# RWKV-7 chain beside attention: the triangular solves of a head pair as one block-diagonal product, and the PSUM bank it leaves given to attention scores

## The chip, the cores and the metric

The kernel runs on one core of a Trainium2 chip. The metric is the device time of one execution in microseconds (us); the median of three executions of the kernel before is 2586.62 us. The engines of a core are called here as the profile calls them: PE (matmuls) with PEld (loads of the stationary operand), DVE, ACT, POOL, and SP, which in this kernel only starts DMA transfers.

## The reference, cut

One layer over 512 latent tokens with 256 context tokens ahead of them: a differential attention of 8 heads and a bidirectional RWKV-7 of 16 heads read the same projected input, are merged, and a PEER layer (retrieval of single-neuron experts) follows. The change concerns the recurrence of RWKV-7 and, by the order of the program, the attention that runs beside it.

```python
def wkv_scan(s0, scan_in):                      # per direction d and head h, 64 x 64 state s
    def step(s, inp):
        w, kk, a, k, v, r = inp
        sa = jnp.einsum('dbhij,dbhj->dbhi', s, kk)
        s = s * w[..., None, :] - sa[..., :, None] * (kk * a)[..., None, :] + v[..., :, None] * k[..., None, :]
        return s, jnp.einsum('dbhij,dbhj->dbhi', s, r)
    return lax.scan(step, s0, scan_in)
...
def one_block(q_blk):                           # attention, 128 queries, all 768 keys
    s = jnp.einsum('bmhqd,bmhkd->bmhqk', q_blk, k).astype(jnp.float32) * scale
    p = jax.nn.softmax(s, axis=-1)
    pd = (p[:, 0] - lam * p[:, 1]).astype(v.dtype)
    return jnp.einsum('bhqk,bhkd->bhqd', pd, v)
...
s_ctx, y_c = wkv_scan(s0, scan_c)               # 256 context tokens, then 512 latent ones
_, y_x = wkv_scan(s_ctx, scan_x)
```

## The kernel before

The program runs in stages: RWKV projections and the operands of the recurrence, pair of heads by pair (to about 715 us), then the recurrence and the attention together (about 743 to 1092 us), the merge of the branches, and PEER to the end.

**The chain.** `rwkv_chain` works through the recurrence in 24 steps of 32 tokens (8 of context, 16 of latent tokens), both directions at once. The 16 heads are 8 pairs; j is the head of a pair, d the direction, and the pairs form two groups g of four. One step has two half-steps, one for each group. A half-step consists of

- `reads` (matmuls L653): 16 products of 128x32 (stationary, from `cb`) with 128x64 (moving, from `sv`) into the bank `ps_r`; ACT copies it to `rhs` (L656);
- `solve` (L663): 16 products of 128x32 (from `XTz`) with 128x64 (`rhs`) into two banks, `ps_u0` and `ps_u1`, one for each j; ACT copies the first to the rows of `sv` that belong to it (L666), DVE the second (L667);
- `state` (L675): 16 products of 128x64 (from `KBt`) with 128x64 (`sv`) into `ps_s`; DVE multiplies it into the `sv` of the next step in two pieces (L681);
- from step 8 on `outputs` (L694, 16 products like those of `reads`, copied by ACT at L697) and `collect` (L705, two transposes, added into `y`).

`XTz` holds the inverse of the triangular system of each pair, head and direction, 32x32, written in stage 1 by `rw_inverse` to `xD`. For each of the four (j, d) there is a tile of 128 rows by 32 columns that is zero outside of its 32 rows, so that a product with all 128 rows of `rhs` gives one solve. `cb` and `KBt` have two buffers, `XTz` two, `sv` three. `load(c + 1)` stands behind the solve of group 0 and `outputs(1, c - 1)`: `cb` and `KBt` are loaded from the SP queue (L637), `sv` (L642) and `XTz` (L644, four loads of 32 rows by 1 KB) from the POOL queue.

**The attention.** A unit is one head and one block of 128 queries: 32 units. `probs` computes four score tiles of 128x384, each from two matmuls (L785, L786) into a bank of the pool `atp` (two banks); DVE scales each into `p` (L788), ACT takes the exponentials (L790). `combine` scales and subtracts (L798 ACT, L800 DVE), transposes six blocks (L804) which ACT copies to `pdT` (L805), and multiplies them with the values (L808, six matmuls). The heads' q and k come through `kr`, `qr`, `va` (`att_load`, POOL queue). Of the 32 units the first 25 take the output bank of the pool `atq`, the last 7 that of `atr`, which opens when the pool of the chain's banks, `psc`, is closed.

**The order.** The two are written one after the other; a scheduler merges them into one fixed order for each engine, by its own model of times. Each engine then runs its row of instructions in that order. A matmul that stands early in PE's row holds up all behind it if its operands are late.

## Time and profile before

| what | value |
|---|---|
| median of 3 executions | 2586.62 us (2585.44 to 2592.0) |
| the profiled execution, its own time | 2591.84 us |
| its span in the trace | 2590.1 us |
| mean granted clock of PE | 0.976 |
| PE busy over the span | 2411.5 us, 93% |
| DVE, ACT, POOL busy | 2025.8 us (78%), 1184.6 us (46%), 482.8 us (19%) |

The profiled execution is 5.2 us above the median. Times of instructions below count from the start of the span. A busy share is an average over stages with different limits, so the stretch of the chain is read by itself: in the rows below it is cut into five pieces at beginnings of steps of the chain. A line of a timeline gives start, duration, engine, line of the program, operation, output and inputs, size, and, where there was any, the idle time before and what ended it. The matmuls of PE overlap, so the time that one takes of PE is read from its start to the start of the next. For the float32 operands here PE runs each matmul as two passes; "x32" in a row are the passes of 16 matmuls, while the transposes are one pass each.

### The profile page before, as it was taken

To read this page: it belongs to the slowest core of one execution; us is meant where nothing else is said; L and a number is where in the kernel's file an instruction comes from. 1 tells how busy PE (TensorE), PEld (TensorE's weight loads), DVE (VectorE), ACT (ScalarE), POOL (GpSimd) and SP (SyncE) were. 2 spreads that over 40 slices of the span, in tenths; PEclk is the share of its full clock that TensorE was granted. 3 is DMA by queue.
4 is the path that set the end of the run, shared out by engine and by line. 5 is a ranking of instruction groups with operands and counts; after the bars stand their busy time and mean duration, and the time that the engine had idled before them with its cause. 6 is when DMAs were issued, how large, how long until landed. Compare 5 with 4: busy or idle time off the path is not lost.

```text
span 2590.1 us, 46535 instructions
## 1 busy us (share of the span) xinstructions
PE 2411.5 (93%) x18109; PEld 2078.5 (80%) x18109; DVE 2025.8 (78%) x3919; ACT 1184.6 (46%) x2171; POOL 482.8 (19%) x518
## 2 busy tenths in 40 slices
PE   6999999899979999899899989998999999988898
PEld 3778778798967878668688979997888998866777
DVE  5779998977748767774499998775778888788894
ACT  4666666633336666652344444552333333323332
POOL 0000000000043333000000000013444444444430
PEclk8999999999989999999899999999999999999999
DMA  5367756787487766235432536779899999899983
GB/s 226 95 164 197 185 149 167 185 264 246 136 210 209 186 175 180 81 102 166 131 109 85 176 130 232 268 284 366 313 336 336 340 339 339 324 363 372 358 327 101
DMA packets 310349, 579.75 MB, mean 224 GB/s; under 512 B 83761, under 2 KB 197041, under 8 KB 303345
## 3 DMA queue, kind: packets, MB, share of 16 engines
q1 hardware_dynamic: 253040, 387.09, 46.6%
q0 software_dynamic: 45808, 155.61, 17.5%
q10 hardware_dynamic: 11280, 34.08, 4.1%
q8 instruction: 142, 2.33, 0.4%
q14 instruction: 79, 0.64, 0.1%
HBM read 470.93 MB, written 105.38 MB: 223 GB/s over the span
## 4 chain that ended last, share of the span: by engine, by line
PE 62%; DVE 20%; DMA 9%; ACT 4%; issue 4%; SPq 0%; POOL 0%; ACTq 0%; DVEq 0%; POOLq 0%
PE ps_v L1143 6%; PE ps_v L1145 6%; PE ps_v L1142 6%; PE ps_a L80 5%; PE ps_a L78 5%; PE ps_a L79 5%; PE pp L79 3%; PE pp L80 3%; PE pp L78 3%; PE ps_s L675 2%; PE ps_br L79 2%; PE ps_br L80 2%; PE ps_br L78 2%; DMA cb<-cbD 2%; PE ps_o L808 2%
## 5 line engine op out<-in xcount | busy, mean ns | idle before, releaser
L78 PE MATMUL ps_a<-h,u_hi 128*128 128x384 f32 x1024 | 346.2, 338 | 10.0 <-ACT u_hi L69 10.0
L80 PE MATMUL ps_a<-h,u_lo 128*128 128x384 f32 x1024 | 347.2, 339 | 7.0 <-DVE u_lo L72 6.7
L79 PE MATMUL ps_a<-h,u_hi 128*128 128x384 f32 x1024 | 344.2, 336 | 0.0
L1080 POOL DMA_INDIRECT gr<-in_peer_u,ei x128 | 165.4, 1292 | 693.1 <-PE ps_a L79 472.5
L69 ACT CAST u_hi<-u_raw 128x1024 fp32r<-128x1024 f32 x128 | 134.3, 1051 | 289.8 <-PE ps_a L79 274.1
L72 DVE TENSOR_TENSOR u_lo<-u_raw,u_hi 128x1024 fp32r<-128x1024 f32 x128 | 156.3, 1221 | 102.4 <-ACT u_hi L69 101.1
L1080 POOL DMA_INDIRECT gr<-in_peer_v,ei x128 | 179.8, 1405 | 203.7 <-DVE ra L1098 182.6
L78 PEld LDWEIGHTS ps_a<-h,u_hi 128*128 128x128 f32 x1024 | 192.8, 188 | 16.1 <-ACT u_hi L69 13.7
L80 PEld LDWEIGHTS ps_a<-h,u_lo 128*128 128x128 f32 x1024 | 192.7, 188 | 12.7 <-DVE u_lo L72 11.6
L79 PEld LDWEIGHTS ps_a<-h,u_hi 128*128 128x128 f32 x1024 | 192.7, 188 | 2.4
L1098 DVE SCALAR_TENSOR_TENSOR ra<-gr,wk,ra 128x1024 f32<-128x1024 f32 x127 | 162.7, 1281 | 2.6 <-DMA gr<-in_peer_v,ei 1.5
L95 ACT CAST w_hi<-w_raw 128x1024 fp32r<-128x1024 f32 (+1 forms) x93 | 106.9, 1149 | 125.1 <-PE ps_br L79 59.3
L96 DVE TENSOR_TENSOR w_lo<-w_raw,w_hi 128x1024 fp32r<-128x1024 f32 (+1 forms) x93 | 125.0, 1344 | 49.5 <-ACT w_hi L95 43.8
L1087 DVE CUSTOM_DVE_ANT_0 gr<-gr,ht 128x1024 f32<-128x1024 f32 x128 | 153.8, 1219 | 11.2 <-DMA gr<-in_peer_u,ei 11.2
L1143 PE MATMUL ps_v<-v_lo,pw_hi 128*128 128x512 f32 x420 | 145.0, 403 | 12.0 <-DVE v_lo L1133 12.0
L1142 PE MATMUL ps_v<-v_hi,pw_hi 128*128 128x512 f32 x420 | 128.5, 400 | 16.0 <-ACT v_hi L1132 16.0
L546 PE MATMUL pp<-At,kz 128*128 128x128 f32 x768 | 106.2, 295 | 35.7 <-DVE kz L539 15.4
L78 PE MATMUL pp<-hx,w_hi 128*128 128x512 f32 x336 | 134.9, 402 | 3.4 <-ACT sgw L433 2.4
L80 PE MATMUL pp<-hx,w_lo 128*128 128x512 f32 x336 | 134.1, 399 | 2.0 <-DVE w_lo L96 2.0
L79 PE MATMUL pp<-hx,w_hi 128*128 128x512 f32 x336 | 133.0, 396 | 1.8 <-DVE hx L231 1.8
L1145 PE MATMUL ps_v<-v_hi,pw_lo 128*128 128x512 f32 x420 | 134.1, 401 | 0.0
L546 PEld LDWEIGHTS pp<-At,kz 128*128 128x128 f32 x768 | 98.4, 207 | 42.9 <-ACT kt L550 18.5
(374 smaller groups left out, 6390.7 us busy)
## 6 DMA issues: line engine op xcount, KB each, us to landing
u_raw<-in_uT SPq DMA_DIRECT2D x128, 512.0 KB, 4.6
v_raw<-in_peer_v SPq DMA_DIRECT2D x70, 512.0 KB, 8.3
w_raw<-in_peer_v SPq DMA_DIRECT2D x58, 512.0 KB, 6.5
wm<-in_w_mod SPq DMA_DIRECT2D x24, 1024.0 KB, 8.8
cb<-cbD SPq DMA_DIRECT2D x48, 512.0 KB, 6.5
gD<-gstage SPq DMA_DIRECT2D x12, 2048.0 KB, 8.3
gg<-gD SPq DMA_DIRECT2D x16, 1536.0 KB, 13.4
actD<-act SPq DMA_DIRECT2D x18, 768.0 KB, 3.6
```

The costliest lines, as they stand in the source:

```text
L69: nc.scalar.copy(hi, raw)
L72: (lo_eng or nc.vector).tensor_tensor(lo, raw, hi.bitcast(F32), op=OP.subtract)
L78: mm(ps, lh[0], rh[0], start=first, stop=False)
L79: mm(ps, lh[0], rh[1], start=False, stop=False)
L80: mm(ps, lh[1], rh[0], start=False, stop=last)
L546: nc.tensor.matmul(ps[:, c, :], kz[:, c, :], at, start=True, stop=True)
L1080: nc.gpsimd.indirect_dma_start(out=r, out_offset=None, in_=self.A[name], in_offset=bass.IndirectOffsetOnAxis(ap=self.ei[:, k:k + 1], axis=0))
L1087: nc.vector.tensor_tensor_reduce(out=r, in0=r, in1=self.ht, scale=1.0, scalar=0.0, op0=OP.mult, op1=OP.add, accum_out=w[:, k:k + 1])
L1098: nc.vector.scalar_tensor_tensor(self.ra, r, w[:, k:k + 1], self.ra, op0=OP.mult, op1=OP.add)
L1142: mm(pc[t][d], w[0][:, ts], v[0][:, c[d]], start=first, stop=False)
L1143: mm(pc[t][d], w[0][:, ts], v[1][:, c[d]], start=False, stop=False)
L1145: mm(pc[t][d], w[1][:, ts], v[0][:, c[d]], start=False, stop=last)
```

## The change

The four solves of a pair, (j, d) in all four combinations, become one product: `XTz` is now a tile in which the four 32x32 inverses of a pair stand on a block diagonal, 128x128, and `solve` has four matmuls of 128x128 with 128x64 instead of 16 of 128x32 with 128x64. The result goes to one PSUM bank, `ps_u`, in which each (j, d) has 32 rows of its own. [...] All that writes or reads operands in that order follows: the order of the halves in `kz`, the rows of `tt`, the mask (built on the host), the loads of `sv`. The two copies of 32x512 out of the solve's banks become four of 32x256, two on ACT (d = 0) and two on DVE (d = 1).

The loads of `XTz` go from 32 rows of 1 KB in one piece to 32 rows of 8 pieces of 128 bytes. The stores of `tt` to `tD` in stage 1 double in number (96 instead of 48, half the size each).

The bank that becomes free goes to the scores: `atp` has three instead of two. `atr`, which opens with the merge, has two instead of three.

```diff
@@ rw_scores
-                            eng.tensor_tensor(zo[:, :, 0, ::-1], zi[:, :, 0], w[1][h, g4], op=OP.mult)
-                            eng.tensor_tensor(zo[:, :, 1], zi[:, :, 1], w[1][h, g4], op=OP.mult)
+                            eng.tensor_tensor(zo[:, :, 1, ::-1], zi[:, :, 0], w[1][h, g4], op=OP.mult)
+                            eng.tensor_tensor(zo[:, :, 0], zi[:, :, 1], w[1][h, g4], op=OP.mult)
...
-                q2 = slice(64 * j + 32, 64 * j + 64)
-                nc.sync.dma_start(tD[j, cc].rearrange("c a d s t -> s (c a d) t"),
-                                  tt[q2].rearrange("p c d t -> p (c d) t"))
+                for dr in range(2):
+                    q = slice(64 * j + 32 - 32 * dr, 64 * j + 64 - 32 * dr)
+                    nc.sync.dma_start(tD[j, cc, :, dr].rearrange("c a s t -> s (c a) t"), tt[q, :, dr])
@@ rwkv_chain
-        clear = lambda j, i: nc.gpsimd.memset(sv[j][i][96 - 64 * j:128 - 64 * j], 0.0)
+        vrow = lambda j, d: slice(64 - 64 * j + 32 * d, 96 - 64 * j + 32 * d)
+        urow = lambda j, d: slice(96 - 64 * j - 32 * d, 128 - 64 * j - 32 * d)
+        clear = lambda j, i: [nc.gpsimd.memset(sv[j][i][urow(j, d), d], 0.0) for d in range(2)]
-        XTz = [mk(f"XTz{i}", [128, 4, 8, 32]) for i in range(NL)]
+        XTz = [mk(f"XTz{i}", [128, 8, 4, 32]) for i in range(NL)]
...
-                    nc.gpsimd.dma_start(sv[j][i][64 - 64 * j:96 - 64 * j, d], self.vTD[t:t + 32, j])
+                    nc.gpsimd.dma_start(sv[j][i][vrow(j, d), d], self.vTD[t:t + 32, j])
-                nc.gpsimd.dma_start(XTz[c % NL][32 * q:32 * q + 32, q], self.xD[q // 2, c, q % 2])
+                nc.gpsimd.dma_start(XTz[c % NL][32 * q:32 * q + 32, :, 3 - q], self.xD[q // 2, c, q % 2])
...
         def solve(g, c):
-            pu = [self.psc.tile([128, 2, 4, 64], F32, name=f"ps_u{j}") for j in range(2)]
-            for dp in range(8):
-                for j in range(2):
-                    q, ur = 2 * j + dp % 2, 96 - 64 * j
-                    nc.tensor.matmul(pu[j][ur:ur + 32, dp % 2, dp // 2, :], XTz[c % NL][:, q, 4 * g + dp // 2, :],
-                                     rhs[g][:, dp // 2, :], start=True, stop=True)
+            pu = self.psc.tile([128, 4, 64], F32, name="ps_u")
+            for a in range(4):
+                nc.tensor.matmul(pu[:, a, :], XTz[c % NL][:, 4 * g + a].rearrange("p u t -> p (u t)"), rhs[g][:, a, :],
+                                 start=True, stop=True)
             G = slice(4 * g, 4 * g + 4)
-            nc.scalar.copy(sv[0][c % NS][96:128, :, G], pu[0][96:128])
-            nc.vector.tensor_copy(sv[1][c % NS][32:64, :, G], pu[1][32:64])
+            for j in range(2):
+                nc.scalar.copy(sv[j][c % NS][urow(j, 0), 0, G], pu[urow(j, 0)])
+                nc.vector.tensor_copy(sv[j][c % NS][urow(j, 1), 1, G], pu[urow(j, 1)])
@@ mixers
-        with self.pool("atp", 2, space=PSUM) as psS, self.pool("atq", 1, space=PSUM) as psO:
+        with self.pool("atp", 3, space=PSUM) as psS, self.pool("atq", 1, space=PSUM) as psO:
...
-                    self.pool("atr", 3, space=PSUM) as psR:
+                    self.pool("atr", 2, space=PSUM) as psR:
```

With these, the scheduler merges chain and attention in another order. The rows below are from the engines' orders; a name's number only tells buffers apart. Lines of the changed program stand three to four higher than before: the score matmuls are L789 and L790, transposes L808, value matmuls L812, reads L657, solve L666, state L679, outputs L698, collect L709.

PE, the second half of step 6 (a context step) before, from the end of the solve of group 1 to the first read of step 7:

```order
L663 MATMUL ps_u_8201<-rhs,XTz_6681 32x64
L663 MATMUL ps_u_8202<-rhs,XTz_6681 32x64
L808 MATMUL ps_o<-va,pdT 128x128 x6
L785 MATMUL ps_s<-kh,q_11246 128x384
L786 MATMUL ps_s<-kl_7297,q_11246 128x384
L785 MATMUL ps_s<-kh,q_11246 128x384
L786 MATMUL ps_s<-kl_7297,q_11246 128x384
L653 MATMUL ps_r<-sv_6688,cb_8149 32x64
```

PE, the second half of a dense context step of the changed program, from its last read to the middle of its `state` pieces:

```order
L657 MATMUL ps_r<-sv_6737,cb_7953 32x64
L679 MATMUL ps_s<-sv_7378,KBt_6732 64x64
L808 MATMUL ps_o<-c_ident,p_11084 128x128 x3
L679 MATMUL ps_s<-sv_7381,KBt_6734 64x64
L679 MATMUL ps_s<-sv_7378,KBt_6732 64x64
L789 MATMUL ps_s<-kh,q_10978 128x384
L790 MATMUL ps_s<-kl_7348,q_10978 128x384
L812 MATMUL ps_o<-va,pdT 128x128 x6
L789 MATMUL ps_s<-kh,q_10978 128x384
L790 MATMUL ps_s<-kl_7348,q_10978 128x384
L679 MATMUL ps_s<-sv_7381,KBt_6734 64x64
```

Before, a context step from 4 to 8 holds five score pairs, two to three groups of three transposes and one group of six value matmuls; now eight, four and two, and `state` is cut into pieces of 1, 2 and 13 by them.

PE, the end of a late step before, outputs of one group to the first read of the next step:

```order
L694 MATMUL ps_r<-sv_6689,cb_10007 32x64
L785 MATMUL ps_s<-kh,q_12070 128x384
L786 MATMUL ps_s<-kl_7297,q_12070 128x384
L804 MATMUL ps_o<-c_ident,p_12176 128x128 x3
L675 MATMUL ps_s<-sv_6688,KBt_6684 64x64
L785 MATMUL ps_s<-kh,q_12070 128x384
L786 MATMUL ps_s<-kl_7297,q_12070 128x384
L705 MATMUL ps_r<-c_ident,yt 128x128 x2
L653 MATMUL ps_r<-sv_6688,cb_10184 32x64
```

The same place of a late step now:

```order
L698 MATMUL ps_r<-sv_6737,cb_9676 32x64
L698 MATMUL ps_r<-sv_6735,cb_9675 32x64
L698 MATMUL ps_r<-sv_6737,cb_9676 32x64
L679 MATMUL ps_s<-sv_6736,KBt_6732 64x64
L709 MATMUL ps_r<-c_ident,yt 128x128 x2
L657 MATMUL ps_r<-sv_6736,cb_9831 32x64
```

From step 18 on the chain runs without attention between its products (one score pair in steps 18 to 22, where there were about six units). Up to the end of step 3 there are 18 value matmuls instead of 12, up to the end of step 9 there are 90 instead of 48, up to the end of step 17 150 instead of 102; when the chain ends 150 stand behind it in both, and 117 score pairs instead of 112.

ACT, in a dense context step now: the second copy of a solve, `sv_6738`, stands behind a copy of transposed probabilities that itself stands behind the first.

```order
L670 COPY sv_6736<-ps_u 32x256
L809 COPY pdT<-ps_o 128x384
L660 COPY rhs<-ps_r 128x256
L809 COPY pdT<-ps_o 128x384
L670 COPY sv_6738<-ps_u 32x256
L761 CAST kh<-kr 128x1536
```

Before, one copy took both directions, and nothing stood between.

## Rows read from the trace of the kernel before

**Rows 1.** The page's part 4: shares of the span on the chain of waits.

```profile
PE 62%; DVE 20%; DMA 9%; ACT 4%; issue 4%; SPq 0%; POOL 0%; ACTq 0%; DVEq 0%; POOLq 0%
```

**Rows 2.** Windows: length, busy PE, PEld, DVE, ACT, POOL; PEclk, DMA share, GB/s.

```profile
743.00:804.35 61.35, 44.80 (x862) 37.36 (x852) 34.61 (x68) 27.20 (x50) 23.40 (x44) 0.89 0.88 226
804.35:858.80 54.45, 53.85 (x1109) 44.91 (x1107) 47.51 (x103) 38.37 (x86) 24.16 (x49) 1.00 0.85 218
858.80:982.26 123.46, 112.46 (x2602) 95.00 (x2601) 82.97 (x180) 76.50 (x190) 44.77 (x88) 0.99 0.68 185
982.26:1056.00 73.74, 72.39 (x1711) 62.57 (x1710) 54.92 (x134) 47.36 (x108) 16.85 (x34) 0.98 0.51 149
1056.00:1092.00 36.00, 31.26 (x192) 24.41 (x192) 25.39 (x68) 26.87 (x67) 0.00 (x0) 1.00 0.23 74
```

**Rows 3.** Timeline of ACT: the `rhs` copy that opens steps 4, 18 and 23.

```profile
804.35 0.37 ACT L656 COPY rhs<-ps_r 128x256 f32<-128x256 f32 x1
...
982.26 0.37 ACT L656 COPY rhs<-ps_r 128x256 f32<-128x256 f32 x1 [2.08 <-PE ps_r L653]
...
1046.55 0.38 ACT L656 COPY rhs<-ps_r 128x256 f32<-128x256 f32 x1
```

**Rows 4.** Timeline of PE: context step 5, and step 19 from reads to outputs.

```profile
815.81 1.09 PE L663 MATMUL ps_u<-rhs,XTz 128*32 128x64 f32 x32
816.82 0.45 PE L785 MATMUL ps_s<-kh,q 128*128 128x384 f32 x1
...
817.28 0.49 PE L804 MATMUL ps_o<-c_ident,p 128*128 128x128 f32 x3
...
823.39 1.60 PE L808 MATMUL ps_o<-va,pdT 128*128 128x128 f32 x12
...
995.88 0.65 PE L653 MATMUL ps_r<-sv,cb 128*32 128x64 f32 x32
996.46 1.15 PE L675 MATMUL ps_s<-sv,KBt 128*64 128x64 f32 x32
997.54 0.55 PE L804 MATMUL ps_o<-c_ident,p 128*128 128x128 f32 x3
...
999.27 0.63 PE L694 MATMUL ps_r<-sv,cb 128*32 128x64 f32 x26
```

**Rows 5.** Timeline of PEld: one load of 128 columns, and two in a row.

```profile
816.82 0.19 PEld L785 LDWEIGHTS ps_s<-kh,q 128*128 128x128 f32 x1
...
823.39 0.30 PEld L808 LDWEIGHTS ps_o<-va,pdT 128*128 128x128 f32 x2
```

**Rows 6.** Timeline of SP's queue: the `cb` loads of steps 19 and 23.

```profile
988.02 0.80 SPq L637 DMA_DIRECT2D cb<-cbD  x2
...
1037.12 1.19 SPq L637 DMA_DIRECT2D cb<-cbD  x2
```

**Rows 7.** DMA issues from 804.35 to 1056: count, KB each, median us to landing.

```profile
cb<-cbD SPq DMA_DIRECT2D x36, 512.0 KB, 6.5
```

**Rows 8.** DMA issues from 1036 to 1044, the last step's loads.

```profile
cb<-cbD SPq DMA_DIRECT2D x2, 512.0 KB, 4.8
```

**Rows 9.** Lines by form, 743 to 1092, DVE, ACT, POOL: busy us, mean ns | idle before.

```profile
L681 DVE TENSOR_TENSOR sv<-ps_s,pcall 64x512 f32<-64x512 f32 x92 | 63.2, 687 | 24.5 <-PE ps_s L675 23.1
L667 DVE COPY sv<-ps_u 32x512 f32<-32x512 f32 x48 | 32.8, 684 | 23.9 <-PE ps_u L663 22.5
L666 ACT COPY sv<-ps_u 32x512 f32<-32x512 f32 x48 | 27.8, 579 | 37.5 <-PE ps_u L663 37.2
L656 ACT COPY rhs<-ps_r 128x256 f32<-128x256 f32 x48 | 17.6, 369 | 21.9 <-PE ps_r L653 17.0 <-DMA qTD<-zt 4.6
L644 POOL DMA_DIRECT2D XTz<-xD x88 | 43.4, 500 | 69.0 <-PE ps_u L663 67.8 <-DMA sv<-vTD 0.9 <-issue 0.2
L751 POOL DMA_DIRECT2D kr<-kTD x14 | 8.3, 598 | 15.2 <-DVE kl L758 15.0 <-issue 0.2
```

**Rows 10.** The page's part 5: gathers issued by POOL in PEER, 128 rows each.

```profile
L1080 POOL DMA_INDIRECT gr<-in_peer_u,ei x128 | 165.4, 1292 | 693.1 <-PE ps_a L79 472.5
```

More of the change, by code (lines that the diff above doesn't have):

```diff
@@ L547, in rw_scores @@
                     for j in range(2):
-                        q = slice(64 * j + 32, 64 * j + 64)
+                        q = slice(64 * j + 32 - 32 * dr, 64 * j + 64 - 32 * dr)
                         nc.scalar.copy(tt[q, c4, dr], ps[q, :, 0:32])
@@ L554, in rw_scores @@
             for j in range(2):
-                q2 = slice(64 * j + 32, 64 * j + 64)
-                nc.sync.dma_start(tD[j, cc].rearrange("c a d s t -> s (c a d) t"),
-                                  tt[q2].rearrange("p c d t -> p (c d) t"))
+                for dr in range(2):
+                    q = slice(64 * j + 32 - 32 * dr, 64 * j + 64 - 32 * dr)
+                    nc.sync.dma_start(tD[j, cc, :, dr].rearrange("c a s t -> s (c a) t"), tt[q, :, dr])
             for dst, src in ((self.cbD[:, 64:192], bt), (self.KBD, kt)):
@@ L1419, in layout @@
     lt, le = (i[:, None] < i[None]).astype(np.float32), (i[:, None] <= i[None]).astype(np.float32)
-    A["mask"] = c(np.stack([np.tile(np.block([[a, b], [0 * lt, le]]), (2, 1))
-                            for a, b in ((lt, le), (lt[::-1], le[::-1]))], axis=1))
+    A["mask"] = c(np.stack([np.tile(np.block(m), (2, 1))
+                            for m in ([[lt, le], [0 * lt, le]], [[0 * lt, le], [lt[::-1], le[::-1]]])], axis=1))
     A["smask"] = c(np.broadcast_to((np.arange(T) % 32 != 0).astype(np.float32), (128, T)))
```

## The prediction, on record before the changed kernel ran

> **What bounds the kernel now.** I read the chain of waits first: 62% of the span is PE, 20% DVE, 9% DMA [rows 1], so that work taken off PE or put on it counts where PE is full. The chain's 349 us I then read in five windows [rows 2]. From 743 to 804 PE is busy 44.8 of 61.4 us while DMA runs at a share of 0.88 and 226 GB/s: loads set the end, and PE has room. In steps 4 to 8 PE is busy 53.85 of 54.45 us, in steps 9 to 17 112.5 of 123.5, from step 18 to the end of the chain 72.4 of 73.7. In the tail it has 4.7 us of room again. A step takes 54.45 / 5 = 10.9 us from 4 to 8, 123.46 / 9 = 13.7 from 9 to 17, and (1046.55 - 982.26) / 5 = 12.9 from 18 to 22 [rows 2, 3]. So the question is not how much faster a solve is, but from where to where the attention moves: out of a stretch where PE is full into others.
>
> **A solve on PE.** Now 16 matmuls take 1.01 us (815.81 to 816.82 [rows 4]), the same number of the same shape in `reads` 0.58 (995.88 to 996.46). Reads go in turn to four bands of 32 output rows, solves to two. By that, a matmul of 64 moving columns costs its own band 0.126 (1.01 / 8) to 0.145 us (0.58 / 4), and four that fill all bands 0.50 to 0.58. Against this stands the load of the stationary operand. Two loads of 128 columns with nothing between them span 0.30 us, a single one 0.19, so one follows another by 0.11 [rows 5]. Four float32 matmuls are eight passes: 8 x 0.11 = 0.88 us. Six matmuls with 128 moving columns take at most 1.60 us [rows 4], 0.267 each, so four with 64 cost no more than 1.07. Bounds 0.50 and 1.07; I take 0.88, since a pass on 64 columns (about half of 0.126) is too short to hide a load of 0.11. Saving 0.13 for a half-step, bounds +0.51 and -0.06.
>
> [...]
>
> **The copies.** One of 32x512 costs 579 ns on ACT and 684 on DVE; one of 256 elements a row 369 on ACT [rows 9]. Two of 256 on ACT are then 0.74, on DVE, taken at 0.40 to 0.42 each by ACT's ratio of the two sizes, 0.82. That adds 0.16 us on ACT and 0.14 on DVE per half-step, 7.5 us in 48 half-steps. It also puts the second copy of ACT behind whatever stands between, in dense steps a `pdT` copy. `state` waits for it, which is why its pieces come as 1, 2 and 13: each cut costs PE about 0.2 us, as pieces overlap less (a passage of 1 or 2 matmuls keeps its own fill and drain). In stretches full of attention these waits are covered by score and value matmuls; in steps 18 to 22 only by outputs and collect.
>
> **The attention that moves.** A pair of score matmuls costs PE 0.46 us (816.82 to 817.28), three transposes 0.3 to 0.5, six value matmuls 1.54 (at most 1.60), reads 0.58, state 1.08, outputs about 0.59 [rows 4]. I sum five stretches.
>
> - A, 743 to step 4: one more unit's values and twelve more score pairs, 12 x 0.46 + 1.54 + 0.3 = 7.4 us of PE work, in a stretch with 16.5 us of room [rows 2] that loads leave. But one more head must be loaded by then, and scores of head 1 wait for it. +4, between -2 and +8.
> - B, steps 4 to 8: per step three more score pairs (1.4), one or two more groups of transposes (0.5), six more value matmuls (1.54), two cuts more (0.4 to 0.5), two cheaper solves (-0.26): 3.7 us, and at the present 1.04 to 1.07 of time over priced work 3.9. PE has no room there, so 5 x 4.0 = +20. DVE's bound is a little lower: its busy time in the five windows adds up to 245.4, less the chain's 63.2 + 32.8 that is 149 for 32 units, 4.7 each [rows 2, 9]; two units 9.3, state 4 x 0.687, copies 4 x 0.41 make 13.7. So a step goes from 10.9 to between 13.7 (+14 in all) and 16.5 (+28), where neither engine hides the other's waits.
> - C, steps 9 to 17: step 9 holds twelve value matmuls instead of six, steps 10 to 17 hold 60 instead of 54, with eight more score pairs and four more groups of transposes: 12/6 x 1.54 + 8 x 0.46 + 4 x 0.35 = 8.2, less 18 cheaper solves (2.3), is 5.9 us, with 11 us of room [rows 2] of which some is waits that stay. Half of it on the path: +3, between -6 and +8.
> - D, step 18 to the end of the chain: some 33 us of attention are gone, and 72.4 us of PE work become about 40. The step does not fall with it, for the loads of `cb` then set it. They have two buffers: a load starts when `outputs` of step c - 1 is done and must land before `reads` of c + 1. From first issue to last landing it takes 0.8 to 1.2 (the two issues) plus 4.8 (last step, nothing else under way) to 6.5 us (the median) [rows 6 to 8], so 5.6 to 7.5; I take 6.5. Then reads, state, solve, outputs in a row: 0.58 + 1.08 + 0.88 + 0.59 and cuts and starts, 3.5 us (4.05 now, 995.88 to the end of outputs [rows 4]). 10.0 a step instead of 12.9, so 5 x -2.9 = -14.5; the last step, 9.45 now, falls by 0.5. -15, between -7 and -23 (8.4 a step, PE's own work and the copies' waits).
> - E, the tail: five score pairs fewer, 5 x 0.46; two output banks instead of three in `atr` take some back. -2, between -3 and +3.
>
> Sum: 4 + 20 + 3 - 15 - 2 = **+10 us**. The profiled execution, 2591.84, would become 2601.8; the median 2586.62 becomes 2596.6, taken as 2597.
>
> At nothing I put the doubled stores of `tt` (half as large each; SP's queue has no share on the chain of waits [rows 1] and `tD` is read a pair later), the split memsets, the other order in `kz` (as many operations of the same size), the mask. What lies behind, merge and PEER, keeps its order and only shifts.
>
> **The XTz loads.** They now have 256 pieces of 128 bytes instead of 32 of 1 KB. POOL takes 0.500 us to issue one, 0.598 for `kr`, which by the code has 128 [rows 9]. A gather of 128 rows takes 1.292, 10.1 ns a row [rows 10]; at that price 256 pieces are 2.6 us. Bounds 0.5 and 2.6 each; I take about 1.0, nearest to `kr`. Four of them then make 4.0, with 2.0 for `sv` (four issues like those of `XTz` now) and about 1 for a head: 7 us of a step of 10, which is hidden.
>
> [...]
>
> **Rivals.**
> 1. *POOL becomes the pace.* At 2.6 us each the loads of a step are 10.4 + 2.0 = 12.4, with a head's 13.5. Steps 4 to 8 (14.9) and 9 to 17 hide that; steps 18 to 22 cannot fall below 12.4, so that D gives back 2.4 x 5 = 12: +22, **2609**. For it: the pieces are eight times as many. Against: `kr`'s issue is hardly dearer than that of `XTz`.
> 2. *The loads get out of the way.* With no head left to load, `cb` lands in 4.8 and PE's own row sets steps 18 to 22 at 8.4: D is -23, the sum +2, **2589**. For it: the last step's loads. Against: `KBt`, `sv` and `XTz` of the same step still come with them.
> 3. *Not slower: the product costs what its bands cost.* At 0.52 a solve, the load being hidden after all, each step saves 0.72 more PE time than I took. B gets 3.6 back, C at 0.9 of it 5.8, A 1, D 2 and half as much for a shorter stall behind `rhs`: 13 together, +10 - 13 = -3, **2584**. With rival 2's loads also true, 2576. It decides from about 0.65 a solve. For it: `reads` against `solve` [rows 4]. Against: loads of 128 columns [rows 5].
>
> **How the numbers follow.** My forecast has 0.50, with its own range 2589 to 2606; POOL 0.10; the loads 0.20; the cheap product 0.20, of which a third with cheap loads. About 0.3%, 7.8 us, is what a measurement of this kernel can tell from no change: the borders are 2578.9 and 2594.4. Of the forecast 0.36 lies above the upper one, 0.12 between, 0.02 below; POOL lies above; of the loads 0.05, 0.12 and 0.03; of the product 0, 0.09 and 0.11. Slower 0.51, same 0.33, faster 0.16. The range reaches from 2577, between the cheap product alone and with cheap loads, to 2613, above POOL's case with B at its dear end.
>
> **What would show it.** Right: step 4 some 4 us later; steps 4 to 8 at about 15 us with PE full; steps 9 to 17 within 8 us of now; steps 18 to 22 at 10 us, PE busy about three quarters, `reads` waiting for `cb`; a solve of 0.9 us to the next start; `XTz` issues of about 1 us. Wrong: steps 4 to 8 below 13.5 (priced work overlaps better than now), steps 18 to 22 at 12 or more (POOL, or a new wait for the second copy) or near 8.4, or a difference before 743 or behind 1092, where I see none.

## The result, and the profile after

The changed kernel takes 2620.89 us (median; 2616.66 to 2626.17), the kernel before 2588.8 in the same comparison: a ratio of 1.0125, with a 95% interval of 1.0097 to 1.0153. It is 32 us slower, where 2597 was forecast and 2613 was the end of the range.

The profiled execution took 2617.17 us, its span is 2615.1. Against the profiled execution before (2591.84) this is 25.3 us; the traces explain this part. The other 7 us lie between executions: the profiled one of before took as long as the slowest of its first three (2592.0), the one of after is near its fastest. In all comparisons below, executions of the kernel before lie between 2574.94 and 2598.70 us.

The windows of the changed kernel, cut at the same steps as [rows 2] (743, step 4, step 9, step 18; the columns are the same). The last row ends at 1082.50, 1.7 us ahead of the end of the last outputs (1084.16), where that of [rows 2] ends with them (1056.00):

```profile
743.00:809.13 66.13, 52.78 (x662) 43.36 (x652) 45.89 (x106) 37.94 (x78) 26.90 (x49) 0.82 0.87 227
809.13:887.22 78.09, 76.39 (x1032) 62.13 (x1033) 65.22 (x160) 62.15 (x141) 30.79 (x56) 1.00 0.66 177
887.22:1010.62 123.40, 123.02 (x2197) 101.58 (x2196) 87.82 (x210) 85.60 (x225) 42.05 (x78) 1.00 0.60 168
1010.62:1082.50 71.88, 59.17 (x1212) 48.10 (x1212) 31.35 (x71) 17.95 (x49) 18.46 (x34) 0.83 0.46 136
```

Against [rows 2]: steps 4 to 8 take 78.09 us instead of 54.45, steps 9 to 17 123.40 instead of 123.46, and PE, which had 11 us of room there, has none. From step 18 to the last outputs it is 73.54 us instead of 73.74, at a granted clock of 0.83 in the row. It has 1242 passes instead of 1711 (30 of them behind the row); 288 of the difference are the solves', which take 8 passes for 32, the rest is attention that went elsewhere. So this stretch lost its attention and hardly any time.

Where the late steps' time goes, by granted clock. Windows of steps 18 to 23 of the changed kernel, cut where the clock changes:

```profile
1010.62:1020.82 10.20, 8.52 (x184) 6.79 (x184) 5.71 (x13) 2.95 (x8) 4.28 (x8) 1.00 0.67 194
1020.82:1034.47 13.65, 11.30 (x172) 9.30 (x176) 3.11 (x7) 2.21 (x6) 3.16 (x6) 0.50 0.42 137
1034.47:1048.13 13.66, 10.51 (x256) 8.61 (x256) 7.69 (x17) 3.69 (x10) 6.68 (x12) 1.00 0.58 165
1048.13:1058.37 10.24, 9.64 (x144) 7.76 (x146) 3.11 (x7) 1.99 (x6) 2.00 (x4) 0.50 0.41 104
1058.37:1082.26 23.89, 19.21 (x466) 15.62 (x462) 11.72 (x27) 6.87 (x20) 2.33 (x4) 1.00 0.35 108
```

Twice the granted clock stands at 0.50, after stretches in which PE was busy 8.52 of 10.20 and 10.51 of 13.66 us; both times it fell while PE waited for `cb`. In the 23.9 us at 0.50 PE does 316 passes, in the 23.9 at 1.00 that follow 466. In the full steps 4 to 17 it is 1.00.

The loop of `cb`, from PE's timeline (reads that waited, or outputs that free the buffer) and SP's:

```profile
1022.91 1.07 PE L657 MATMUL ps_r<-sv,cb 128*32 128x64 f32 x30 [2.58 <-DMA cb<-cbD]
...
1029.25 1.06 PE L698 MATMUL ps_r<-sv,cb 128*32 128x64 f32 x26
...
1048.46 1.08 PE L657 MATMUL ps_r<-sv,cb 128*32 128x64 f32 x30 [1.92 <-DMA cb<-cbD]
...
1062.47 0.65 PE L657 MATMUL ps_r<-sv,cb 128*32 128x64 f32 x30 [1.08 <-DMA cb<-cbD]
```

```profile
1014.66 0.80 SPq L641 DMA_DIRECT2D cb<-cbD  x2
...
1030.21 0.80 SPq L641 DMA_DIRECT2D cb<-cbD  x2
...
1041.35 1.01 SPq L641 DMA_DIRECT2D cb<-cbD  x2
...
1055.77 0.80 SPq L641 DMA_DIRECT2D cb<-cbD  x2
```

From the issue at 1014.66 to the reads at 1022.91 are 8.25 us, from there to the next issue 7.30, at the granted clock of 0.50. In the next turn the reads come at 1036.23, 6.02 us after the issue, and do not wait for the load: until then PE is busy with the rest of the step, most of it at 0.50. From these reads to the next issue are 5.12 us, at 1.00. The three loads that reads waited for in the five steps took 8.25, 7.11 (to 1048.46) and 6.70 us (to 1062.47); the section from reads to the next issue took 4.7 to 5.1 us at 1.00 and 7.3 at 0.50. Why 5.1, where I had put 3.5, is seen on PE in step 20:

```profile
1036.23 0.65 PE L657 MATMUL ps_r<-sv,cb 128*32 128x64 f32 x32
1036.82 0.33 PE L679 MATMUL ps_s<-sv,KBt 128*64 128x64 f32 x2
1037.08 0.30 PE L698 MATMUL ps_r<-sv,cb 128*32 128x64 f32 x2
1037.82 0.34 PE L679 MATMUL ps_s<-sv,KBt 128*64 128x64 f32 x4 [0.45 <-ACT sv L670]
1038.09 0.31 PE L698 MATMUL ps_r<-sv,cb 128*32 128x64 f32 x4
1038.32 1.03 PE L679 MATMUL ps_s<-sv,KBt 128*64 128x64 f32 x26
1039.28 1.10 PE L666 MATMUL ps_u<-rhs,XTz 128*128 128x64 f32 x8
1040.32 0.63 PE L698 MATMUL ps_r<-sv,cb 128*32 128x64 f32 x26
1040.90 0.31 PE L679 MATMUL ps_s<-sv,KBt 128*64 128x64 f32 x2
```

`state` and `outputs` come in pieces, since they need four copies that end one after the other; for ACT's second PE stands still 0.45 us. From 1036.82 to the solve pass 2.46 us (with six passes of outputs), where state in one piece takes 1.08 [rows 4]. The rest of the 5.12 is reads (0.59), solve (1.04), outputs (0.58), and 0.45 until SP, which issues `KBt` until 1041.25, issues the load. In the other half of the same step nearly nothing is cut (two passes of state stand ahead), and state, outputs and solve take 2.60 us, where they take 4.08 above:

```profile
1042.43 1.15 PE L679 MATMUL ps_s<-sv,KBt 128*64 128x64 f32 x30
1043.50 0.65 PE L698 MATMUL ps_r<-sv,cb 128*32 128x64 f32 x32
1044.09 1.10 PE L666 MATMUL ps_u<-rhs,XTz 128*128 128x64 f32 x8
1045.03 0.39 PE L709 MATMUL ps_r<-c_ident,yt 128*128 128x128 f32 x2
```

So the solve takes 0.94 us to the next start where transposes follow it and 1.04 where outputs do, against 1.01 before. Before, PE ran solve and outputs in part at once, as this place of step 19 in the trace before shows (solve from 998.37, outputs from 999.08 between its last passes, all done when the scores start):

```profile
998.37 0.92 PE L663 MATMUL ps_u<-rhs,XTz 128*32 128x64 f32 x26
999.08 0.25 PE L694 MATMUL ps_r<-sv,cb 128*32 128x64 f32 x2
...
999.83 0.44 PE L785 MATMUL ps_s<-kh,q 128*128 128x384 f32 x1
```

Both together took 1.46 us. Now they take 1.53 in the half that is not cut, and 1.62 in the other, with six of 32 output passes done before. In the rows of step 20 the eight passes of a solve stand in one piece, with no pass of outputs between them. What was lost by this is small: before, 1.46 us for both, where 1.01 for a solve and 0.59 for outputs, each by itself, make 1.60; now the 1.53 are 0.94 and 0.59.

What the pieces cost as a whole is seen in PE's busy time in one line, summed over all five windows. Changed kernel, state (L679), outputs (L698), solve (L666):

```profile
sum 375.00, PE 81.11 PEld 63.04; mean PE 16.22 PEld 12.61
```

```profile
sum 375.00, PE 33.94 PEld 22.09; mean PE 6.79 PEld 4.42
```

```profile
sum 375.00, PE 57.36 PEld 50.86; mean PE 11.47 PEld 10.17
```

Before, the same three (L675, L694, L663):

```profile
sum 349.00, PE 65.45 PEld 54.72; mean PE 13.09 PEld 10.94
```

```profile
sum 349.00, PE 26.63 PEld 19.99; mean PE 5.33 PEld 4.00
```

```profile
sum 349.00, PE 59.05 PEld 50.93; mean PE 11.81 PEld 10.19
```

The solve gains 1.7 us in the whole chain, `state` loses 15.7 and `outputs` 7.3. Of these, 5.2 and 4.8 lie behind the start of step 18, where the granted clock fell (0.83 in that row above); the rest lies in stretches at a clock of 1.00 and ahead of step 4.

POOL's issues and the copies (lines by form, 743 to 1092 for POOL, to 1118 for the others, columns as in [rows 9]):

```profile
L648 POOL DMA_DIRECT2D XTz<-xD x88 | 51.4, 591 | 78.3 <-PE ps_u L666 58.9 <-PE ps_r L709 17.4 <-issue 2.1
```

```profile
L670 ACT COPY sv<-ps_u 32x256 f32<-32x256 f32 x96 | 35.0, 365 | 53.5 <-PE ps_u L666 46.9 <-DVE sv L671 5.2
```

```profile
L671 DVE COPY sv<-ps_u 32x256 f32<-32x256 f32 x96 | 39.9, 415 | 41.4 <-ACT sv L670 40.1
```

### The profile page after: what moved, and what is told of

Its sections match the earlier page's. It is cut to its first block, busy times and chain, and to the rows that moved or that the text cites. A ratio compares the mean times of both kernels' runs of the same rounds, so it can differ in the third digit from the quotient of the medians.

```text
span 2615.1 us, 44424 instructions
## 1 busy us (share of the span) xinstructions
PE 2434.4 (93%) x16957; PEld 2088.0 (80%) x16957; DVE 2028.4 (78%) x3967; ACT 1190.8 (46%) x2219; POOL 495.7 (19%) x524
## 4 chain that ended last, share of the span: by engine, by line
PE 59%; DVE 20%; DMA 10%; issue 5%; ACT 5%; POOL 1%; SPq 1%; ACTq 0%; DVEq 0%; POOLq 0%
PE ps_v L1147 5%; PE ps_v L1149 5%; PE ps_v L1146 5%; PE ps_a L80 5%; PE ps_a L78 5%; PE ps_a L79 5%; PE pp L79 3%; PE pp L78 3%; PE pp L80 3%; PE ps_s L679 2%; DMA v_raw<-in_peer_v 2%; PE ps_br L80 2%; PE ps_br L79 2%; PE ps_br L78 2%; PE ps_u L666 2%
## 5 line engine op out<-in xcount | busy, mean ns | idle before, releaser
L78 PEld LDWEIGHTS ps_a<-h,u_hi 128*128 128x128 f32 x1024 | 192.8, 188 | 16.1 <-ACT u_hi L69 13.7
L1091 DVE CUSTOM_DVE_ANT_0 gr<-gr,ht 128x1024 f32<-128x1024 f32 x128 | 153.9, 1220 | 11.8 <-DMA gr<-in_peer_u,ei 11.6
```

The costliest lines, as they stand in the source:

```text
L78: mm(ps, lh[0], rh[0], start=first, stop=False)
L1091: nc.vector.tensor_tensor_reduce(out=r, in0=r, in1=self.ht, scale=1.0, scalar=0.0, op0=OP.mult, op1=OP.add, accum_out=w[:, k:k + 1])
```

## The experiments

Two theories stood against each other. M: attention was moved into full steps, and the late steps it left cannot pay this back, since the loop of `cb` and the granted clock hold them. P: the product with its copies is dearer wherever it stands. All times are medians; ratios are to the kernel before in the same comparison, with their 95% intervals.

**Product alone, bank alone.** e1 takes the third score bank back:

```diff
-        with self.pool("atp", 3, space=PSUM) as psS, ...
+        with self.pool("atp", 2, space=PSUM) as psS, ...
-                    self.pool("atr", 2, space=PSUM) as psR:
+                    self.pool("atr", 3, space=PSUM) as psR:
```

> The changed kernel with two score banks and three in atr, as before: the block-diagonal product, its copies and loads alone. Steps 4 to 8 now hold 60 - 18 = 42 value matmuls instead of 60 in the changed kernel and 30 before, and only steps 21 and 22 are empty of attention. Theory M (attention moved into full steps, and the emptied steps 18 to 22 do not pay it back, for the loads of cb and the granted clock hold them): steps 4 to 8 at 11.7 to 12.7 us instead of 15.6, so that much of the loss goes: 2593 to 2603. Theory P (the product with its four copies is dearer wherever it stands, a fixed sum for each of the 48 half-steps): 2614 to 2622, as the changed kernel.

Measured: 2616.06, 1.0117 (1.0087 to 1.0147). Steps 4 to 8 take 66.4 us, after 78.1 less of a fall than M asked for, and steps 9 to 17 take 133.3, steps 18 to 22 66.1. Steps 4 to 17 take 199.7 us in e1 and 201.5 in the changed kernel, though 18 value matmuls fewer are done by then: with two score banks PE waits 4.4 us in steps 4 to 8 and 4.7 in 9 to 17. Steps 21 and 22 are empty and take 13.9 and 10.9 us, at a granted clock of 0.79. Attention ends 3.6 us later than in the changed kernel. So the forecast of M missed: the product, with the order that came with it, brings nearly the whole loss without the third bank.

e2 is the kernel before with three score banks, its solves in one shared bank:

```diff
-            pu = [self.psc.tile([128, 2, 4, 64], F32, name=f"ps_u{j}") for j in range(2)]
+            pu = [self.psc.tile([128, 2, 4, 64], F32, name="ps_u")] * 2
```

> The kernel before with its 16 matmuls a solve, both heads of a pair in one bank (their rows do not overlap), and the bank so gained given to the scores: three in atp, two in atr. Steps 4 to 8 hold 54 - 12 = 42 value matmuls, steps 18 to 22 36, about as before. Theory M: a little of the same, steps 4 to 8 at about 12.5 us instead of 10.9 (+8), the later steps shorter by nearly that: 2587 to 2598. Theory P: the bank costs nothing, 2585 to 2592; so this run tells only whether a third bank by itself can bring the 32 us, which neither theory expects.

Measured: 2598.13, 1.0045 (1.0026 to 1.0063), at the upper end of M's range. Steps 4 to 8 take 63.5 us, 9 more than before, steps 9 to 17 117.9, 5.6 less.

**The late steps filled.** e3 lets all 32 units use the bank of `atq`, so that the seven units that waited for the end of the chain stand in steps 17 to 22:

```diff
-                self.attention(b1, wk, psS, [psO] * 25 + [psR] * 7, ld)
+                self.attention(b1, wk, psS, [psO] * 32, ld)
```

> The changed kernel with the output bank of atq for all 32 units, so that the seven units which waited for the end of the chain stand in steps 17 to 22 (42 value matmuls, 12 score pairs). Theory M: the idle time of PE in steps 18 to 22 takes them in: a step stays at 12.5 to 13.2 us, at a granted clock of 1.00 instead of 0.83, and the tail behind the chain falls from 35 to about 17 us: 2598 to 2606. Theory P: each of these steps is set by its products and copies, so that the attention adds to it and only what is idle for cb (7 us in all) is gained: 2611 to 2618.

Measured: 2590.06, 1.0014 (0.9996 to 1.0032). The median falls by 31 us with this one line, more than either theory said, and the interval takes in the kernel before. Windows of steps 4 to 8, 9 to 17 and 18 to 22 of e3, and of the end of its chain:

```profile
813.60:891.70 78.10, 76.41 (x1032) 62.14 (x1033) 65.20 (x160) 62.14 (x142) 30.77 (x56) 1.00 0.68 177
891.70:1014.70 123.00, 123.00 (x2201) 101.74 (x2199) 87.46 (x207) 85.38 (x224) 41.83 (x77) 1.00 0.60 168
1014.70:1079.90 65.20, 64.28 (x1213) 53.50 (x1215) 40.63 (x107) 35.90 (x95) 18.68 (x35) 1.00 0.54 150
1079.90:1098.00 18.10, 10.74 (x182) 7.76 (x178) 9.93 (x24) 5.06 (x12) 0.00 (x0) 0.72 0.15 40
```

Steps 4 to 17 are those of the changed kernel to 0.4 us; steps 0 to 3 take 2.8 us more. Steps 18 to 22 take 65.2 instead of 62.8 us with 42 value matmuls more in them; PE is busy 64.28, at a clock of 1.00. Seven units cost 2.4 us there, and attention ends with step 22 instead of 46 us behind its end. So the late steps had room for work that the changed kernel does behind the chain. In the profiled executions, 20.7 of the 29.6 us between the two stand where the merge begins (1122.27, 1101.61); the other 8.9 stand nearly all behind it, and the traces do not show that e3 caused them.

e4 does the same to the kernel before.

> The kernel before with the output bank of atq for all 32 units; solves, banks and copies as before. It completes the square of product and free late units. If room in late steps is what the free units use, there is little here (1.4 us idle in steps 18 to 22), and only the last step and the tail can gain: 2580 to 2588. If the free units by themselves are worth what they gave in the changed kernel (31 us), 2556 to 2565.

Measured: 2598.58, 1.0043 (1.0026 to 1.0059); both expectations missed. The late steps are full there, so that none of the freed units moved into them, and behind the chain all share one output bank: from the chain's end to the end of attention 43.3 us instead of 33.2. Here, free units are worth something only where the steps have room.

**The loop of `cb`.** e6 puts `cb` in one tile for each group, each loaded when its own outputs are done, half a step earlier for group 0:

```diff
+        def load_cb(g, c):
+            cb = cbs[g, c] = [b1.tile([128, 8, 64], F32, name=f"cb{j}{g}", bufs=NL) for j in range(2)]
...
             outputs(0, c)
+            if c < 22:
+                load_cb(0, c + 2)
             solve(1, c)
```

> The changed kernel with cb in two tiles, one for each group, each loaded as soon as its own group's outputs of two steps earlier are done: the tile of group 0 starts half a step earlier. Theory M, loads as what holds the empty steps: steps 18 to 22 fall from 12.6 to 9 to 10 us if the clock comes back, to about 11 if it stays at half in stretches; 2603 to 2613, and nothing changes in steps 4 to 8. Theory P: nothing waits for cb that would not wait for copies: 2617 to 2623.

Measured: 2609.33, 1.0088 (1.0057 to 1.0119), as M said. Windows of its steps 18 to 22, one each:

```profile
1011.70:1020.90 9.20, 8.58 (x214) 7.16 (x214) 5.54 (x13) 2.95 (x9) 3.86 (x9) 1.00 0.74 186
1020.90:1030.10 9.20, 8.39 (x214) 6.96 (x213) 5.39 (x13) 2.94 (x8) 4.33 (x9) 1.00 0.79 219
1030.10:1039.20 9.10, 8.39 (x214) 6.96 (x213) 5.39 (x13) 2.94 (x8) 4.32 (x9) 1.00 0.75 201
1039.20:1050.10 10.90, 8.65 (x214) 7.06 (x213) 5.70 (x13) 2.96 (x9) 6.04 (x11) 1.00 0.88 234
1050.10:1063.00 12.90, 12.54 (x214) 10.32 (x213) 5.16 (x12) 2.96 (x9) 0.00 (x0) 0.61 0.34 94
```

The same 214 passes take 9.1 to 9.2 us with loads that come in time, 10.9 with 1.5 us of idle time ahead of the reads (the profile names no releaser), 12.9 at the clock of 0.61. The five steps are 11.5 us shorter than in the changed kernel, so that the loop of `cb` held them there; a part of this is clock, 0.90 instead of 0.81 over the five steps. What the clock costs is seen in the last row: 3.7 us in one step.

**The clock.** e5 fills the waits of the changed kernel's late steps with repeated products, three times 16 a step, e15 those of e6 with two times 16:

```diff
+            if 17 <= c < 23:
+                dup(c)
```

> The changed kernel with 48 matmuls more at the end of each of the steps 17 to 22, a repetition of products of outputs whose result nobody reads, where PE waits for cb. Theory M with the clock: in the changed kernel PE's work in steps 18 to 22 takes 52.1 us for what takes 39.3 before, at a granted clock of 0.83; with the wait filled the clock stays at 1.00, the five steps fall from 62.8 to 54 to 58 us in spite of 1.9 us more work in each, and the time to 2612 to 2617. If the clock is not what lengthens these steps, the added work lengthens them: 2620 to 2628.

Measured: 2618.82, 1.0120 (1.0095 to 1.0146), between the two ranges. The clock fell all the same (0.83 from step 19 to 22, PE busy 44.8 of 51.2 us), so that e5 says nothing of what a held clock is worth.

> e6 (cb by groups) with 32 matmuls more in each of the steps 17 to 22, a repetition of products of outputs whose result nobody reads. In e6 a step of these took 9.1 to 9.2 us at a granted clock of 1.00 and 12.9 at 0.61, with the same 107 matmuls. If PE's idle time is what lets the clock fall, and the filled steps hold it: five steps of 9.7 to 10.2 us, 49 to 51 in all, no longer than e6's 51.2 in spite of 1.1 us more work in each; 2605 to 2611. If the clock falls all the same: 55 to 58 us for the five, 2612 to 2617.

Measured: 2619.81, 1.0133 (1.0104 to 1.0162), above both ranges. Steps 18 to 22:

```profile
1016.00:1070.50 54.50, 50.12 (x1386) 41.08 (x1386) 26.75 (x61) 14.77 (x41) 17.36 (x32) 1.00 0.64 168
```

Here the clock held, at 50.12 us busy of 54.50, but the added products stand in the way of the chain: 10.2 to 11.8 us a step instead of 9.2. My 1.1 us for them was too little, and the time is no better. In the late steps the granted clock was 1.00 with PE busy 64.28 of 65.20 us (e3) and 50.12 of 54.50 (e15), 0.90 with 46.56 of 51.30 (e6) and 0.83 with 44.8 of 51.2 (e5). In these four, more idle time goes with a lower clock; but in the tail of the kernel before it was 1.00 with 31.26 of 36.00 [rows 2], so that what lets it fall is not shown. Filling with work that is thrown away gained nothing.

**The cuts.** e8 lets the first half of `state` need only the first copy of each engine:

```diff
-            for dp in range(8):
+            for k in range(8):
                 for j in range(2):
+                    dp = 2 * (k % 4) + (j + k // 4) % 2
...
-                nc.vector.tensor_copy(sv[j][c % NS][urow(j, 1), 1, G], pu[urow(j, 1)])
+                nc.vector.tensor_copy(sv[1 - j][c % NS][urow(1 - j, 1), 1, G], pu[urow(1 - j, 1)])
```

> The changed kernel with another order of the products of state and of DVE's two copies: the first eight products need only the first copy of either engine, the last eight the second ones, so that state comes in pieces of 8 and 8 instead of 1, 2 and 13. If the cuts are what makes state dearer in the changed kernel (72.9 us of PE time against 60.3 before, some 8 of the difference at full clock), state falls to 62 to 66 us and the time to 2608 to 2615; if it is the interleaving with products of other shapes at all, nothing changes: 2618 to 2623.

Measured: 2615.0, 1.0119 (1.0093 to 1.0145), the upper end. `state` came in pieces of 8 and 8 or 1, 7 and 8, but the scheduler also put other attention beside it (steps 4 to 8 are 70.0 us instead of 78.1), so that the 6 us are not the cuts' alone.

> The order of e8 and the output bank of e3 for all 32 units together. If both gains are PE time where PE is full, they add up: 2577 to 2585, below the kernel before (2586.5). If the cuts cost nothing once the steps are filled: 2587 to 2592, as e3.

Measured: 2592.0, 1.0026 (1.0010 to 1.0042): the gains of e3 and e8 do not add up.

**Without the product.** e10 is e2 with all units free.

> The old 16 products a solve in one shared bank, three score banks, and the output bank of atq for all 32 units: e3 without the product. In e2 steps 18 to 22 are nearly full (2.9 us idle), so that there is little room for more units before the chain's end: 2590 to 2598, no better than e3. If it is below 2585, the product is a loss even where attention fills the late steps.

Measured: 2588.19, 1.0009 (0.9992 to 1.0026), 2 us below the range. With the late steps filled, the product (e3) and the old solves (e10) do not differ beyond their intervals: in this setting the product is worth nothing.

**`cb` by groups elsewhere.** On the kernel before (e13), on e10 (e11) and on e9 (e12):

> The kernel before with cb in two tiles by group, as in e6. PE waits 7.1 us for cb in steps 9 to 22 of the kernel before. If the loop of cb costs its waits there and no more: 2578 to 2584. If what is won is lost again where PE is full: 2585 to 2589.

Measured: 2588.17, 0.9997 (0.9985 to 1.0010): the 7.1 us of waits did not come back.

> Old solves in one bank, three score banks, all 32 units free (e10), and cb by groups. PE is idle 5.8 us in steps 9 to 17 of e10, 1.8 in 18 to 22. 2580 to 2586 if these were waits for cb, 2587 to 2590 if not.

Measured: 2592.56, 1.0011 (0.9997 to 1.0025), above both ranges: no gain either.

> The product with its other order of state and all units free (e9), and cb by groups. PE is idle 4.0 us in steps 9 to 17 and 0.6 in 18 to 22 of e9, but 12.9 before step 4. 2586 to 2592 as e9 if only late loads change, 2580 to 2586 if the first steps gain too.

Measured: 2585.28, 0.9988 (0.9974 to 1.0003): with the product it gains against e9, and is level with the kernel before. The gain lies mostly ahead of the late steps, which were full in e9: by the traces, step 4 begins 3.0 us earlier, steps 9 to 17 are 4.0 us shorter and steps 18 to 22 1.5. Why the same split gains here and not in e11 and e13 is not shown.

**A version below both.** e14 is e12 with two score banks and three in `atr`, as before.

> The product with the other order of state, all units free and cb by groups (e12), but two score banks and three in atr as before: the third bank undone in the best of the versions with the product. If the third bank is what moves attention into the first steps and gains nothing where every step is full: 2578 to 2586, no slower than e12 (2585.3), with steps 0 to 4 shorter than e12's 63.8 us. If three banks keep DVE and PE from waiting for each other in full steps: 2590 to 2598.

Measured: 2573.91, 0.9961 (0.9939 to 0.9982), below both ranges. Its windows, cut as those of the changed kernel:

```profile
748.50:810.00 61.50, 53.43 (x626) 42.88 (x626) 44.11 (x100) 37.52 (x76) 25.65 (x47) 0.78 0.85 217
810.00:881.00 71.00, 68.52 (x977) 57.41 (x977) 56.44 (x135) 50.38 (x117) 26.76 (x49) 0.95 0.71 181
881.00:999.90 118.90, 117.37 (x2186) 98.19 (x2186) 88.54 (x207) 85.13 (x220) 47.73 (x87) 1.00 0.73 184
999.90:1059.00 59.10, 59.10 (x1207) 50.83 (x1208) 46.16 (x121) 36.91 (x97) 18.12 (x34) 1.00 0.60 162
1059.00:1088.00 29.00, 25.42 (x278) 17.91 (x276) 17.85 (x42) 16.61 (x42) 0.00 (x0) 1.00 0.28 92
```

The late steps are full (59.10 of 59.10 us) and take 11.2 us each but for the first (14.3), and the attention ends at 1088 instead of 1092.5. So 4.5 of its 18 us in the profiled execution lie in chain and attention. The rest lies behind, where the program is that of before; how much of that is the version's, the traces do not say.

Nor do chain and attention show what undoing the third bank brought. e12 and e14 begin the merge at the same time and come apart behind it, in the stage that uses `atr`, the pool that gave up a bank (times from the start of the span; in brackets from the merge's first transposes):

| kernel | banks in `atr` | first transposes of the merge | first `ps_mu` | first gather of PEER |
|---|---|---|---|---|
| before | 3 | 1095.62 | 1106.62 (11.0) | 1736.00 (640.4) |
| changed | 2 | 1122.27 | 1135.94 (13.7) | 1763.89 (641.6) |
| e12 | 2 | 1091.16 | 1105.17 (14.0) | 1733.52 (642.4) |
| e14 | 3 | 1090.97 | 1101.80 (10.8) | 1726.83 (635.9) |

In all 18 traces the first bracket is 10.5 to 11.0 with three banks in `atr` and 12.7 to 14.8 with two, the second 635.7 to 640.4 and 640.6 to 645.0. So what the third score bank costs e12 is seen between the merge and PEER's first gather, 6.5 us. The traces have another 4.8 behind it, without a cause that they show. The medians differ by 11.4 us; the intervals of the two ratios touch.

e16 takes the product out of it, e17 the free units.

> e14 without the product: the kernel before, with cb by groups and all 32 units free; two score banks, 16 products a solve. Here 144 value matmuls are done at the end of step 22, in e14 168, so eight units and not four stand behind the chain, on one output bank. If the product is what makes room for e14's gain: 2588 to 2600 (e4 without the split of cb had 2598.6). If cb by groups and the free units are the gain, whatever the solve: 2570 to 2580.

Measured: 2588.76, 1.0010 (0.9999 to 1.0022): without the product the same settings gain nothing. By the traces its merge begins at 1109.25, 18.3 us later than that of e14.

> e14 with the limit of 25 units that may run beside the chain, as in the changed kernel: product, order of state, cb by groups, two score banks. Steps 20 to 22 are empty of attention. If the emptied late steps are what costs: 2595 to 2607, with a fallen clock in steps 20 to 23 and a tail of 45 us instead of 29. If the third bank was the cost in the changed kernel and the free units are a small matter: 2574 to 2584.

Measured: 2584.53, 0.9999 (0.9986 to 1.0013), at the end of the second range. It empties the end of the chain again, and there the clock falls again (0.94 in steps 18 to 22, 0.89 behind); the time from the start of step 23 to the end of attention is 47.8 us instead of 29.0. This costs 10.6 us against e14, not the 21 to 33 that I expected; by the traces the merge begins 15.8 us later (1106.80). That is also 11.2 us later than before (1095.62), so only the whole time is level with the kernel before, not chain and attention: in the traces the stretch behind is 13.7 us shorter (1480.8 instead of 1494.5 us from the first transposes). So the limit of 25 units did harm, of 11 to 16 us in this setting; in the changed kernel filling the late steps gave 31.

## Why the prediction was wrong, by its steps

The direction was right, and most of the loss stands where it was forecast, in steps 4 to 8; the gain that was to pay for it did not come. Terms of the sum, forecast and profiled execution:

| term | forecast | measured | from |
|---|---|---|---|
| A, 743 to step 4 | +4 (-2 to +8) | +4.8 | 804.35 to 809.13 |
| B, steps 4 to 8 | +20 (+14 to +28) | +23.6 | 54.45 to 78.09 |
| C, steps 9 to 17 | +3 (-6 to +8) | -0.1 | 123.46 to 123.40 |
| D, step 18 to the chain's end (1059.3, 1085.9) | -15 (-7 to -23) | -1.7 | 77.0 to 75.3 |
| E, from there to the end of attention | -2 (-3 to +3) | 0 | 33.2 to 33.2 |
| sum | +10 | +26.6 | the profiled executions differ by 25.3 |

**The step that failed is D**, outside of its own bounds. I priced a late step as a load of 6.5 us (5.6 to 7.5) and a section of 3.5, together 10.0; the five steps took 12.6 each. The loads that reads waited for took 6.7, 7.1 and 8.3, the last outside the bounds; the section took 4.7 to 5.1 at the granted clock of 1.00 and 7.3 at 0.50. Two things were left out. First, I summed the section from products in one piece, though the order printed with the change showed `state` cut, and though I had myself said that in steps 18 to 22 the waits for the second copies are covered by outputs and collect alone. In step 20, state with its cuts, a wait of 0.45 us and six passes of outputs takes 2.46 us where I had put 1.08, and the solve 0.16 more; the sections at 1.00 are 1.2 to 1.6 us too long for this. The outputs, which I had put behind the solve, took the 0.59 that I gave them. Second, I took PE's busy share of about three quarters as harmless: the granted clock, 0.98 to 1.00 in the other windows of [rows 2], fell twice to 0.50, each time in a wait for `cb`, and two of five sections took 2.2 to 2.6 us more for it. [rows 2] had a hint: 0.89 in the first window, the one with the most idle time of PE (16.55 of 61.35 us). The sign that I had named for this, steps 18 to 22 at 12 us or more, came; of the two causes that I had named with it, POOL is out, and waits for the second copy are 1.6 us in the whole stretch.

**B was right in mechanism**, 3.6 us too small. The 0.2 us for a cut was my estimate: a piece of `state` of two passes takes 0.26 us to the next start (1036.82), where two of the 32 in one piece come to 0.07. I had priced two cuts a step at 2.0 to 2.5 us in all: PE's busy time in state is 17.26 us there instead of 12.62, +4.6. Outputs, which begin in step 8, add 0.9.

**The solve** takes 0.94 to 1.04 us from start to start, near the 0.88 of the forecast and inside its bounds of 0.50 and 1.07. The third rival, a product at the price of its bands, is gone. The 0.88 were eight loads at 0.11 [rows 5], an estimate; the trace has 0.06 to 0.16 more, and no run shows what fills them.

**POOL** issues an `XTz` load in 591 ns, below my 1.0 us and far from 2.6: the first rival is out. **The copies** cost 365 ns on ACT and 415 on DVE, as forecast.

**The second rival**, loads out of the way, was wrong for the change, whose late steps take 12.6 us and not 8.4. It comes near in e6, where `cb` is loaded earlier and three of the late steps take 9.1 to 9.2.

**What the sum missed as a whole** is that the late steps were worth more filled than emptied. Seven units stand behind the chain in both kernels; before, the late steps had no room for them (e4). In the changed kernel they have: e3 puts the seven units there for 2.4 us, and the 46 us of attention behind step 22 go. No term of the sum asked whether the emptied steps could be filled again.

**Behind the chain** I saw no difference. With two banks instead of three in `atr` the first `ps_mu` comes 2.7 us later behind the merge's first transposes; the whole stretch behind these is 1492.8 us instead of 1494.5, so that this does not decide the outcome.

Open: the 7 us between profiled executions and medians; the length of the stretch behind the merge's first transposes, 1480.8 (e17) to 1496.6 us (e5) in the traces, of which the banks of `atr` explain a part, so that the times of e14 and e17 are not those of chain and attention alone; and the product apart from the order that the scheduler gives with it, for no run has the one without the other.

## What to carry to other kernels

When an edit makes a scheduler move filler work forward, price the place that it leaves as well as the one it goes to: here an emptied stretch did not shrink to its own work, for the loop of its loads, its chain of small waits and the granted clock (0.83) held it, at 12.6 us a step. The block-diagonal product had a quarter of the instructions and was hardly cheaper (0.94 to 1.04 us instead of 1.01), and the four copies that take its result out cut the products behind it into pieces. Where an empty stretch shows in the order, look for the limit that keeps work out of it (here a list of 25 units) before the resource that the edit offers. When a bank goes from one pool to another, read the stage that loses it too.

## What the runs showed of the hardware that I had not expected

The same 214 passes of one chain step took 9.1 us at a granted clock of 1.00 and 12.9 at 0.61 (e6). In the changed kernel the granted clock fell to 0.50 after stretches in which PE was still busy 8.52 of 10.20 and 10.51 of 13.66 us; it was 1.00 in stretches with 50.12 of 54.50 (e15) and 64.28 of 65.20 (e3). Products of 32 columns ran in part beside each other on PE: solve and outputs together took 1.46 us, the solve alone 1.01 and the outputs alone 0.59. A piece of `state` of two passes took 0.26 us to the next start, where all 32 in one piece take 1.08.
